# Routing chain of a mixture-of-experts kernel: transposing the residual raw, with norm factor and modulation moved behind the gather

## The chip, the cores and the metric

The kernel runs on one core of a Trainium2 chip. Its time is the device time of one execution in microseconds (us). The matrix engine is TensorE (PE; its weight loads are PEld), the others are VectorE (DVE), ScalarE (ACT) and GpSimd (POOL); SyncE (SP) issues the weight transfers. SBUF is the memory the engines work from, PSUM holds matmul results in eight tiles of 128 x 512 float32.

## The reference

Two layers act on 256 tokens of width 1024 and 256 context tokens. The first mixes with a gated MLP and a convolution and has a dense feed-forward part. The second has windowed attention and a mixture of eight experts, of which each token takes two. The change lies in the second layer, between the attention's residual and the experts:

```python
hl = rms_norm(xl, norm_ffn_g[li]) * (1 + sc2) + sh2
...
logits = (h @ router).astype(jnp.float32)
vals, idx = lax.top_k(logits, TOP_K)
wts = jax.nn.softmax(vals, axis=-1)
...
for e in range(N_EXPERTS):
    y = y + combine[..., e:e + 1] * swiglu(h, w1[e], w3[e], w2[e])
```

So the normalised value of token n and feature d is x[n,d] times a factor r[n] of the token, times a factor and plus a shift that depend on the feature alone.

## The kernel before

The program is a list of steps, written out in the order in which every engine is to issue; each engine works through its own part of that order. Weights come in pieces of 1 MB ("granules") from SP's queue into raw buffers, ten at most here, and are issued as soon as a buffer is free. A granule of a float32 matmul in three passes is first split: ScalarE casts it (L233), VectorE subtracts the cast from it (L211), and `mm3` (L262 to L264) multiplies high by high, high by low and low by high parts. The splitting runs up to three granules ahead.

The residual lies feature-major: `xt[k]` holds 128 features by 512 tokens, its first 256 columns are the latent tokens. `wo` (four steps) adds the attention's output to it, collects the squares and multiplies the raw residual with the prepared router weights (`logits`, L1276). Then four steps follow: an ada granule pair (modulation vectors of the layer's last part, L371), `route_a`, another pair, `route_b`.

`route_a` ends the logits and the norm: `SumSq.finish` sums over features on TensorE (L310), takes the reciprocal root on VectorE (L269 to L275) and multiplies it into two diagonal matrices (L316). `route_b` spreads the factor to all partitions with these (L321), scales the logits and takes the two best experts per token on VectorE (L1320 to L1331). Five small matmuls (L1334 to L1338) count, for each token and expert, the chosen tokens before it, and the total per expert; all write one PSUM tile. Eight times, VectorE multiplies a tile of the residual with the factor (L1343) and ScalarE applies scale and shift (L1345) into the unused half of `xt`. After the fourth of these, the rank is copied out (L1347), the one-hots for the first expert are built (L1440: place number equal to rank, times selection), and the order of the experts by size is worked out (`order_a`) and read into SP's registers (`order_load`), since it decides which weights are fetched next. Then sixteen 128 x 128 transposes (L1359) make the tokens lie on partitions, copied out (L1360) into `htok`.

`gather(n)` selects an expert's tokens by matmuls of `htok` with the one-hots (L1492): two halves of four feature blocks, 32 instructions in all, each half in one PSUM tile. ScalarE casts a half into the high part of `xg` (L1495), VectorE subtracts to get the low part (L1496). `gather(0)` stands in `route_b`; it is called again ahead of each of the three other experts with 128 places. The four experts with 64 places are served by one `gather_small` (L1505, L1506). For the large experts `eh` and `ey` run in three passes; the small ones use raw weights (L1550, L1607). In the sequence, pieces of a large and of a small expert alternate. Behind the last step stands a loop for the case that an expert has more tokens than places.

Of the kernel before, what the change touches and what calls it, by code (L numbers as in the profile page):

```python
# [22 lines left out]
F32 = mybir.dt.float32  # L23
# [4 lines left out]
AF = mybir.ActivationFunctionType  # L28
ALU = mybir.AluOpType
AX = mybir.AxisListType  # L30

P = 128
D = 1024
KD = 8
T = 512
L = 256
FF = 3584
NFG = 7
E = 8
# [47 lines left out]
def build(ctx, tc, io):  # L87
    nc = tc.nc
    ve, se, te = nc.vector, nc.scalar, nc.tensor
# [3 lines left out]
    cp = ctx.enter_context(tc.tile_pool(name="cp", bufs=1))  # L93
# [4 lines left out]
    pools = {"s": phase.enter_context(tc.tile_pool(name="sp", bufs=SB, side="right"))}  # L98
# [4 lines left out]
    cnt = [0]  # L103
# [5 lines left out]
    def S(dtype=F32):  # L109
        return pools["s"].tile([P, 512], dtype, tag="s", name=nm("s"))  # L110
# [7 lines left out]
    def PS():  # L118
        return pp.tile([P, 512], F32, tag="p", name=nm("p"))
# [7 lines left out]
    f32 = lambda ap: ap.bitcast(F32)  # L127


    vecs = cp.tile([P, NV], F32, name="vecs")  # L130
    ident = cp.tile([P, P], F32, name="ident")
    xt = [xp.tile([P, 512], F32, tag="xt", name=f"xt{k}") for k in range(KD)]
    cst = cp.tile([P, NK], F32, name="cst")
    rows = cp.tile([P, R_BS], F32, name="rows")
    router = cp.tile([P, KD, E], F32, name="router")
    ones = cp.tile([P, P], F32, name="ones")
# [8 lines left out]
    Affn = [cp.tile([P, KD, 2], F32, name=f"af{l}") for l in range(2)]  # L145
    SH1, SC1, G1, SH2, SC2, G2 = (8 * i for i in range(6))

    def mod(l, c, s):
        q = mpos(c)
        return modT[l][:, q, s:s + 1]  # L150
# [127 lines left out]
    def rsqrt(v, n):  # L278
        y = tiny(n)
        for op in rsqrt_ops(v, n, y):  # L280
            op()
        return y

    class SumSq:
# [17 lines left out]
        def add(self, src):  # L302
            self.accum(self.square(src))

        def finish(self):

            nt = self.n // P
            ps = PS()
            for t in range(nt):
                te.matmul(ps[:, t:t + 1], lhsT=self.acc[:, t * P:(t + 1) * P], rhs=ones[:, 0:1], start=True, stop=True)  # L310
            v = tiny(nt)
            ve.tensor_scalar(v, ps[:, :nt], 1.0 / D, EPS, op0=ALU.mult, op1=ALU.add)
            self.r = rsqrt(v, nt)
            self.dg = S()
            for t in range(nt):
                ve.tensor_scalar(self.dg[:, t * P:(t + 1) * P], ident, self.r[:, t:t + 1], None, op0=ALU.mult)  # L316
# [11 lines left out]
    C = {}  # L328
# [975 lines left out]
    def route_a(_):  # L1304
        logits(6)
        logits(7)
        C["ss"].finish()

    def route_b(_):
        pb = C["ss"].bcast()  # L1310
        r = C["ss"].r
        iota8 = iota[:, :E]
        sel = cp.tile([P, 2, E], F32, name="sel")
        comb = cp.tile([P, 2, E], F32, name="comb")
        rank = cp.tile([P, 2, E], F32, name="rank")
        lgs = tiny(16).rearrange("p (t e) -> p t e", t=2)
        mx = tiny(16).rearrange("p (t e) -> p t e", t=2)
        ix = tiny(16, U32).rearrange("p (t e) -> p t e", t=2)
        for t in range(2):
            ve.scalar_tensor_tensor(lgs[:, t, :], C["lg"][t][:, :E], r[:, t:t + 1], C["c0"], op0=ALU.mult, op1=ALU.add)  # L1320
            ve.max(mx[:, t, :], lgs[:, t, :])
            ve.max_index(ix[:, t, :], mx[:, t, :], lgs[:, t, :])
        del C["lg"]
        xf = tiny(4).rearrange("p (t c) -> p t c", t=2)
        ve.tensor_copy(xf, ix[:, :, 0:2])
        o0 = tiny(16).rearrange("p (t e) -> p t e", t=2)
        o1 = tiny(16).rearrange("p (t e) -> p t e", t=2)
        for t in range(2):
            ve.tensor_scalar(o0[:, t, :], iota8, xf[:, t, 0:1], None, op0=ALU.is_equal)
            ve.tensor_scalar(o1[:, t, :], iota8, xf[:, t, 1:2], None, op0=ALU.is_equal)  # L1330
        ve.tensor_add(sel, o0, o1)  # L1331
        tri = cst[:, K_TRI:K_TRI + P]
        ps = PS()
        te.matmul(ps[:, 0:E], lhsT=tri, rhs=sel[:, 0, :], start=True, stop=True)  # L1334
        te.matmul(ps[:, E:2 * E], lhsT=tri, rhs=sel[:, 1, :], start=True, stop=False)
        te.matmul(ps[:, E:2 * E], lhsT=ones, rhs=sel[:, 0, :], start=False, stop=True)
        te.matmul(ps[:, 2 * E:3 * E], lhsT=ones, rhs=sel[:, 0, :], start=True, stop=False)
        te.matmul(ps[:, 2 * E:3 * E], lhsT=ones, rhs=sel[:, 1, :], start=False, stop=True)  # L1338

        hn = []  # L1340
        for k in range(KD):
            t = S()
            ve.tensor_mul(t[:, :L], xt[k][:, :L], pb[:, :L])  # L1343
            hn.append(xt[k][:, L:])
            se.activation(hn[k], t[:, :L], AF.Identity, bias=mod(1, SH2 + k, 0), scale=Affn[1][:, k, 0:1])  # L1345
            if k == 3:
                ve.tensor_copy(rank, ps[:, 0:2 * E].rearrange("p (t e) -> p t e", t=2))  # L1347
                C["sel"], C["comb"], C["rank"] = sel, comb, rank
                onehots(0)
                cnt = C["cnt"] = cp.tile([P, E], F32, name="cnt")  # L1350
                ve.tensor_copy(cnt, ps[:, 2 * E:3 * E])
                order_a()
                order_load()
        htok = C["htok"] = pools["t"].tile([P, 2, D], F32, tag="htok", name="htok")
        for hf in range(2):
            for t in range(2):
                pt = PS()
                for k in range(4):
                    te.transpose(pt[:, k * P:(k + 1) * P], hn[4 * hf + k][:, t * P:(t + 1) * P], ident)  # L1359
                (se.copy if t else ve.tensor_copy)(htok[:, t, hf * 512:(hf + 1) * 512], pt)  # L1360
        gather(0)
        flush_tails()

        w = tiny(6).rearrange("p (c t) -> p c t", t=2)
        ve.tensor_sub(w[:, 0, :], mx[:, :, 1], mx[:, :, 0])
        se.activation(w[:, 0, :], w[:, 0, :], AF.Exp)
        ve.tensor_scalar(w[:, 1, :], w[:, 0, :], 1.0, None, op0=ALU.add)
        ve.reciprocal(w[:, 1, :], w[:, 1, :])
        ve.tensor_mul(w[:, 2, :], w[:, 0, :], w[:, 1, :])
        for t in range(2):  # L1370
            ve.tensor_scalar(o0[:, t, :], o0[:, t, :], w[:, 1, t:t + 1], None, op0=ALU.mult)
            ve.scalar_tensor_tensor(comb[:, t, :], o1[:, t, :], w[:, 2, t:t + 1], o0[:, t, :], op0=ALU.mult, op1=ALU.add)
# [48 lines left out]
    def order_load():  # L1421

        _, C["ex"] = nc.values_load_multi_w_load_instructions(
            C["exi"][0:1, :], engines=[mybir.EngineType.SP], min_val=1, max_val=E - 1)
        state["stop"] = None
        issue_dma()
# [8 lines left out]
    def onehots(n):  # L1435

        sel, _, rank = column(n)
        oh = S()
        for t in range(2):
            ve.tensor_scalar(oh[:, t * P:(t + 1) * P], iota, rank(t), sel(t), op0=ALU.is_equal, op1=ALU.mult)  # L1440
        C["oh"] = [oh[:, t * P:(t + 1) * P] for t in range(2)]
# [41 lines left out]
    def gather(n):  # L1483

        oh = C.pop("oh")
        xg = pools["t"].tile([P, 2, KD, P], F32R, tag="xg", name=nm("xg"))
        for hf in range(2):
            ps = PS()
            for kk in range(4):
                k = 4 * hf + kk  # L1490
                for t in range(2):
                    te.matmul(ps[:, kk * P:(kk + 1) * P], lhsT=C["htok"][:, t, k * P:(k + 1) * P], rhs=oh[t],  # L1492
                              start=(t == 0), stop=(t == 1), skip_group_check=True)
            pv = ps.rearrange("p (k c) -> p k c", k=4)
            se.copy(xg[:, 0, 4 * hf:4 * hf + 4, :], pv)  # L1495
            ve.tensor_sub(xg[:, 1, 4 * hf:4 * hf + 4, :], pv, f32(xg[:, 0, 4 * hf:4 * hf + 4, :]))  # L1496
        C["xg"] = [(xg[:, 0, k, :], xg[:, 1, k, :]) for k in range(KD)]

    def gather_small(_):

        oh = C.pop("ohs")
        for k in range(KD):
            ps = PS()
            for t in range(2):
                te.matmul(ps[:, :L], lhsT=C["htok"][:, t, k * P:(k + 1) * P], rhs=oh[t], start=(t == 0), stop=(t == 1))  # L1505
            se.copy(xt[k][:, L:], ps[:, :L])  # L1506

    ada(1, 10, quiet=True, late=True)
    step(route_a, quiet=True)
# [221 lines left out]
    with tc.If(cv > 0):  # L1731
        for t in range(2):
            ve.tensor_sub(rank[:, t, :], rank[:, t, :], C["slots"])
        with tc.For_i(0, E, 1) as ei:
# [17 lines left out]
            for k in range(KD):  # L1752
                ps = PS()
                for t in range(2):
                    te.matmul(ps[:, :P], lhsT=htok[:, t, k * P:(k + 1) * P], rhs=oh[:, t * P:(t + 1) * P],
                              start=(t == 0), stop=(t == 1))
                ve.tensor_copy(xg[k // 4][:, (k % 4) * P:(k % 4 + 1) * P], ps[:, :P])
            yp = [PS(), PS()]
            for fg in range(NFG):
                hp = []  # L1760
# [153 lines left out]
```

## Time and profile before

| | us |
|---|---|
| median of three runs | 1869.96 (1869.2 to 1872.01) |
| the profiled execution, its own time | 1878.57 |
| its span, first to last instruction | 1876.7 |

| engine | busy us | share of span |
|---|---|---|
| TensorE matmuls | 1785.8 | 95% |
| TensorE weight loads | 1300.2 | 69% |
| VectorE | 1133.6 | 60% |
| ScalarE | 768.1 | 41% |
| GpSimd | 438.7 | 23% |

Times in the rows below are from the start of the span. A busy share is an average over stages with different limits, so the stages have to be looked at one by one. An engine's wait is put down to whatever released it last.

### The profile page before, as it was taken

The page shows a single profiled execution, that of the slowest core. Times are in us where ns is not written, and L with a number is a line of the kernel's source. Part 1 is how long each engine was busy: PE and PEld are TensorE (multiplying, and loading weights), DVE is VectorE, ACT ScalarE, POOL GpSimd, SP SyncE. Part 2 cuts the span into 40 slices and gives each one's busy share as a digit, 9 for nine tenths or more (in the row PEclk, how much of TensorE's full clock was granted, in tenths as well). Part 3 has the DMA queues.
Part 4 walks back from the last instruction along what each step waited for, and adds up shares of the span by engine and source line. Part 5 has one row for each costly group of instructions (what it writes and reads, how often), then busy time and mean ns, then how long its engine had stood idle before and what let it go on. Part 6 is the DMA issues. An engine that isn't in the chain of part 4 may idle for free.

```text
span 1876.7 us, 24027 instructions
## 1 busy us (share of the span) xinstructions
PE 1785.8 (95%) x9438; PEld 1300.2 (69%) x9438; DVE 1133.6 (60%) x1598; ACT 768.1 (41%) x851; POOL 438.7 (23%) x188
## 2 busy tenths in 40 slices
PE   5999999999999999987989999999999999999998
PEld 4889878788888888886587656565656565656553
DVE  5788874378977521568757555655555545555553
ACT  4545543432222222254736444444443444444441
POOL 1587446245444444416600000000000000000000
PEclk8999999999999999998999999999999999999999
DMA  8542144554544422250076999999999999999994
GB/s 337 183 148 77 60 159 155 197 186 155 181 160 153 157 90 90 93 199 23 2 314 249 406 419 420 361 421 401 419 420 375 392 421 419 416 365 412 404 420 183
DMA packets 71686, 489.99 MB, mean 261 GB/s; under 512 B 8080, under 2 KB 9488, under 8 KB 13200
## 3 DMA queue, kind: packets, MB, share of 16 engines
q1 hardware_dynamic: 70992, 487.88, 65.9%
q8 instruction: 76, 1.25, 0.3%
q10 hardware_dynamic: 576, 0.52, 0.1%
q14 instruction: 42, 0.34, 0.1%
HBM read 487.32 MB, written 1.05 MB: 260 GB/s over the span
## 4 chain that ended last, share of the span: by engine, by line
PE 70%; DMA 12%; DVE 10%; ACT 4%; issue 3%; POOL 0%; SPq 0%; DVEq 0%; ACTq 0%; POOLq 0%
PE p L262 18%; PE p L264 17%; PE p L263 17%; DMA raw<-in_moe 9%; PE p L1550 8%; DVE lo L211 3%; PE p L1607 2%; ACT hi L233 2%; DMA q<-in_moe 2%; DVE p L569 1%; PE p L1570 1%; DVE s L300 1%; PE p L1176 1%; PE p L371 1%; PE p L1157 1%
## 5 line engine op out<-in xcount | busy, mean ns | idle before, releaser
L211 POOL TENSOR_TENSOR lo<-raw,hi 128x2048 fp32r<-128x2048 f32 (+1 forms) x68 | 309.4, 4553 | 426.1 <-ACT hi L233 406.9
L233 ACT CAST hi<-raw 128x2048 fp32r<-128x2048 f32 x172 | 327.7, 1907 | 188.4 <-PE p L264 80.3
L262 PE MATMUL p<-s,hi 128*128 128x512 f32 x960 | 376.2, 392 | 0.7 <-ACT s L434 0.7
L263 PE MATMUL p<-s,hi 128*128 128x512 f32 x960 | 374.8, 390 | 1.4 <-DVE s L764 1.1
L264 PE MATMUL p<-s,lo 128*128 128x512 f32 x960 | 374.5, 390 | 0.6 <-POOL lo L205 0.6
L211 DVE TENSOR_TENSOR lo<-raw,hi 128x2048 fp32r<-128x2048 f32 (+1 forms) x108 | 244.9, 2269 | 80.0 <-ACT hi L233 80.0
L211 DVE TENSOR_TENSOR lo<-q,hi 128x2048 fp32r<-128x2048 f32 x70 | 160.2, 2292 | 217.0 <-ACT hi L233 217.0
L233 ACT CAST hi<-q 128x2048 fp32r<-128x2048 f32 x70 | 133.4, 1907 | 187.9 <-DMA q<-in_moe 132.6
L262 PEld LDWEIGHTS p<-s,hi 128*128 128x128 f32 x960 | 180.9, 188 | 40.0 <-ACT s L434 0.9
L263 PEld LDWEIGHTS p<-s,hi 128*128 128x128 f32 x960 | 180.8, 188 | 39.8 <-DVE s L764 1.7
L264 PEld LDWEIGHTS p<-s,lo 128*128 128x128 f32 x960 | 180.8, 188 | 38.6 <-POOL lo L205 1.1
L264 PE MATMUL p<-hi,xg 128*128 128x512 f32 x448 | 176.8, 395 | 5.4 <-DVE xg L1496 5.4
L262 PE MATMUL p<-hi,xg 128*128 128x512 f32 x448 | 180.6, 403 | 0.0
L263 PE MATMUL p<-lo,xg 128*128 128x512 f32 x448 | 176.9, 395 | 2.2 <-DVE lo L211 2.1
L262 PE MATMUL p<-hi,s 128*128 128x256 f32 (+1 forms) x480 | 164.8, 343 | 1.6 <-ACT s L434 1.6
L263 PE MATMUL p<-lo,s 128*128 128x256 f32 (+1 forms) x480 | 160.8, 335 | 0.0
L397 DVE SCALAR_TENSOR_TENSOR s<-raw,o 128x512 f32<-128x512 f32 x128 | 158.8, 1303 | 0.0
L1550 PE MATMUL p<-q,xt 128*64 128x512 f32 x552 | 153.1, 613 | 0.0
L446 DVE SCALAR_TENSOR_TENSOR xt<-p,mod,xt 128x256 f32<-128x256 f32 x216 | 90.3, 476 | 76.9 <-PE p L264 69.6
L569 DVE SCALAR_TENSOR_TENSOR p<-s,vecs,p 128x494 f32<-128x494 f32 (+11 forms) x192 | 125.8, 732 | 6.2 <-ACT p L551 6.2
L264 PE MATMUL p<-hi,s 128*128 128x512 f32 (+1 forms) x352 | 123.7, 351 | 0.0
L262 PEld LDWEIGHTS p<-hi,s 128*128 128x128 f32 x480 | 92.3, 192 | 31.8 <-issue 21.9
(251 smaller groups left out, 2193.9 us busy)
## 6 DMA issues: line engine op xcount, KB each, us to landing
raw<-in_moe SPq DMA_DIRECT2D x181, 1024.0 KB, 10.2
q<-in_moe SPq DMA_DIRECT2D x153, 1024.0 KB, 14.0
raw<-in_ff SPq DMA_DIRECT2D x42, 1024.0 KB, 4.8
raw<-in_ada SPq DMA_DIRECT2D x31, 1024.0 KB, 5.8
raw<-in_adaT SPq DMA_DIRECT2D x16, 1024.0 KB, 4.8
raw<-in_w_ag SPq DMA_DIRECT2D x8, 1024.0 KB, 6.6
raw<-in_w_uv SPq DMA_DIRECT2D x8, 1024.0 KB, 4.8
raw<-in_w_out SPq DMA_DIRECT2D x6, 1024.0 KB, 4.8
```

The source lines that it names most:

```text
L211: eng.tensor_sub(lo[:, sl], r[:, sl], f32(hi[:, sl]))
L233: se.copy(hi, raws[i])
L262: te.matmul(out, lhsT=lh[0], rhs=rh[0], start=first, stop=False, skip_group_check=True)
L263: te.matmul(out, lhsT=lh[0], rhs=rh[1], start=False, stop=False, skip_group_check=True)
L264: te.matmul(out, lhsT=lh[1], rhs=rh[0], start=False, stop=last, skip_group_check=True)
L300: ve.tensor_add(self.acc[:, :n], self.acc[:, :n], q[:, :n])
L371: te.matmul(ps[32 * j:32 * j + 32, :P], lhsT=cpad[:, k, :], rhs=rv[:, kk, j * P:(j + 1) * P], start=(k == 0), stop=(k == 7), skip_group_ch ...
L397: ve.scalar_tensor_tensor(j, g[0][:, jj * D + q * 512:jj * D + (q + 1) * 512], 1.0, C["cb"][s][q], op0=ALU.mult, op1=ALU.mult, accum_out=h ...
L446: ve.scalar_tensor_tensor(xt[d][:, sl], ps[:, sl], mod(l, gbase + d, s), xt[d][:, sl], op0=ALU.mult, op1=ALU.add)
L569: ve.scalar_tensor_tensor(ov[:, :, lo:hi], gv[:, :, lo + s:hi + s], vecs[:, w0 + j:w0 + j + 1], ov[:, :, lo:hi], op0=ALU.mult, op1=ALU.add)
L1550: te.matmul(ps[SMALL * z:SMALL * (z + 1), :], lhsT=xt[k][:, o:o + SMALL], rhs=w[z][:, kk, :], start=(k == 0), stop=(k == 7), skip_group_ch ...
L1607: te.matmul(yps[n][SMALL * z:SMALL * (z + 1), :], lhsT=hT[:, f * SMALL:(f + 1) * SMALL], rhs=w[:, ff, z * 512:(z + 1) * 512], start=(fg == ...
```

## The change

The residual is transposed raw, at the start of `route_b`; the norm's factor is multiplied into the selection (`selr`), from which all one-hots are built; scale and shift are applied to the gathered rows. The diagonals and the spreading matmul are no longer made on this path. Counting is done by four matmuls, the totals in a PSUM tile of their own. In `gather` the modulation is made twice from the PSUM tile: by ScalarE into the high part, by VectorE in float32 into an SBUF tile `v`, from which the high part is subtracted. A filler of 448 bytes per partition and the new `selr` (64 bytes) shift later tiles by 512 bytes.

```diff
+    cp.tile([P, 112], F32, name="pad")
...
-        def finish(self):
+        def finish(self, diag=True):
...
             self.r = rsqrt(v, nt)
+            if not diag:
+                return
...
-        C["ss"].finish()
+        C["ss"].finish(diag=False)
+
+    def modulated(o, ps, k):
+
+        se.activation(o, ps, AF.Identity, bias=mod(1, SH2 + k, 0), scale=Affn[1][:, k, 0:1])
 
     def route_b(_):
-        pb = C["ss"].bcast()
         r = C["ss"].r
+        htok = C["htok"] = pools["t"].tile([P, 2, D], F32, tag="htok", name="htok")
+        for hf in range(2):
+            for t in range(2):
+                pt = PS()
+                for k in range(4):
+                    te.transpose(pt[:, k * P:(k + 1) * P], xt[4 * hf + k][:, t * P:(t + 1) * P], ident)
+                se.copy(htok[:, t, hf * 512:(hf + 1) * 512], pt)
...
+        selr = cp.tile([P, 2, E], F32, name="selr")
...
-        ps = PS()
-        te.matmul(ps[:, 0:E], lhsT=tri, rhs=sel[:, 0, :], start=True, stop=True)
-        te.matmul(ps[:, E:2 * E], lhsT=tri, rhs=sel[:, 1, :], start=True, stop=False)
-        te.matmul(ps[:, E:2 * E], lhsT=ones, rhs=sel[:, 0, :], start=False, stop=True)
-        te.matmul(ps[:, 2 * E:3 * E], lhsT=ones, rhs=sel[:, 0, :], start=True, stop=False)
-        te.matmul(ps[:, 2 * E:3 * E], lhsT=ones, rhs=sel[:, 1, :], start=False, stop=True)
-
-        hn = []
-        for k in range(KD):
-            t = S()
-            ve.tensor_mul(t[:, :L], xt[k][:, :L], pb[:, :L])
-            hn.append(xt[k][:, L:])
-            se.activation(hn[k], t[:, :L], AF.Identity, bias=mod(1, SH2 + k, 0), scale=Affn[1][:, k, 0:1])
...
+        ps, pc = PS(), PS()
+        te.matmul(ps[:, 0:2 * E], lhsT=tri, rhs=sel.rearrange("p t e -> p (t e)"), start=True, stop=False,
+                  skip_group_check=True)
+        te.matmul(ps[:, E:2 * E], lhsT=ones, rhs=sel[:, 0, :], start=False, stop=True, skip_group_check=True)
+        te.matmul(pc[:, 0:E], lhsT=ones, rhs=sel[:, 0, :], start=True, stop=False)
+        te.matmul(pc[:, 0:E], lhsT=ones, rhs=sel[:, 1, :], start=False, stop=True)
+        for t in range(2):
+            ve.tensor_scalar(selr[:, t, :], sel[:, t, :], r[:, t:t + 1], None, op0=ALU.mult)
+        ve.tensor_copy(rank, ps[:, 0:2 * E].rearrange("p (t e) -> p t e", t=2))
+        C["sel"], C["comb"], C["rank"] = selr, comb, rank
+        onehots(0)
+        cnt = C["cnt"] = cp.tile([P, E], F32, name="cnt")
+        ve.tensor_copy(cnt, pc[:, 0:E])
+        order_a()
+        order_load()
         gather(0)
         flush_tails()
...
-            pv = ps.rearrange("p (k c) -> p k c", k=4)
-            se.copy(xg[:, 0, 4 * hf:4 * hf + 4, :], pv)
-            ve.tensor_sub(xg[:, 1, 4 * hf:4 * hf + 4, :], pv, f32(xg[:, 0, 4 * hf:4 * hf + 4, :]))
+            v = S()
+            for kk in range(4):
+                k, pk = 4 * hf + kk, ps[:, kk * P:(kk + 1) * P]
+                modulated(xg[:, 0, k, :], pk, k)
+                ve.tensor_scalar(v[:, kk * P:(kk + 1) * P], pk, Affn[1][:, k, 0:1], mod(1, SH2 + k, 0), op0=ALU.mult,
+                                 op1=ALU.add)
+            ve.tensor_sub(xg[:, 1, 4 * hf:4 * hf + 4, :], v.rearrange("p (k c) -> p k c", k=4),
+                          f32(xg[:, 0, 4 * hf:4 * hf + 4, :]))
...
-            se.copy(xt[k][:, L:], ps[:, :L])
+            modulated(xt[k][:, L:], ps[:, :L], k)
```

The loop behind the last step gets `modulated` in place of its copy as well.

## Rows read from the trace of the kernel before

**Rows 1.** Stretches: us, busy time (instructions) per engine, TensorE clock, DMA share, GB/s.
```profile
970.00:989.20 19.20, 14.43 (x131) 12.14 (x131) 11.40 (x51) 6.05 (x12) 0.00 (x0) 0.73 0.59 229
...
1200.00:1300.00 100.00, 99.48 (x458) 62.08 (x458) 55.60 (x44) 41.87 (x33) 0.00 (x0) 1.00 0.95 384
1300.00:1400.00 100.00, 93.94 (x428) 55.13 (x426) 57.77 (x43) 46.57 (x35) 0.00 (x0) 1.00 1.01 419
```

**Rows 2.** Timeline, 969 to 985: start, us, what, count, [idle before, releaser].
```profile
971.68 1.08 PE L371 MATMUL p<-q,cpad 128*32 128x128 f32 x32
...
973.09 0.48 DVE L316 TENSOR_SCALAR s<-ident,t 128x128 f32<-128x128 f32 x2
...
976.27 0.59 PE L1334 MATMUL p<-sel,cst 128*128 128x8 f32 x2 [1.94 <-DVE sel L1331]
...
978.00 0.57 PE L1338 MATMUL p<-sel,ones 128*128 128x8 f32 x2
...
978.61 0.17 DVE L1347 COPY rank<-p 128x16 f32<-128x16 f32 x1 [1.07 <-PE p L1338]
978.82 0.60 DVE L1440 TENSOR_SCALAR s<-cst,rank,sel 128x128 f32<-128x128 f32 x2
...
984.51 13.23 SPq L185 DMA_DIRECT2D q<-in_moe  x4
...
984.88 4.46 PE L1492 MATMUL p<-s,htok 128*128 128x128 f32 x32
```

**Rows 3.** Timeline, from the first gather to the first weight subtractions.
```profile
989.20 0.47 PE L262 MATMUL p<-hi,xg 128*128 128x512 f32 x1
...
989.99 0.69 DVE L1496 TENSOR_TENSOR xg<-p,xg 128x512 fp32r<-128x512 f32 x1 [1.09 <-ACT xg L1495]
...
990.97 3.70 ACT L233 CAST hi<-q 128x2048 fp32r<-128x2048 f32 x2
...
992.89 6.70 DVE L211 TENSOR_TENSOR lo<-q,hi 128x2048 fp32r<-128x2048 f32 x3 [0.42 <-ACT hi L233]
```

**Rows 4.** Timeline around the gather of the second large expert.
```profile
1187.91 3.73 PE L1492 MATMUL p<-s,htok 128*128 128x128 f32 x32
...
1190.48 0.59 ACT L1495 CAST xg<-p 128x512 fp32r<-128x512 f32 x1
...
1190.98 2.28 DVE L211 TENSOR_TENSOR lo<-raw,hi 128x2048 fp32r<-128x2048 f32 x1
...
1193.92 0.50 PE L264 MATMUL p<-hi,xg 128*128 128x512 f32 x1 [1.81 <-DVE xg L1496]
```

**Rows 5.** The chain of waits, same place: start, us, what.
```profile
1193.18 0.69 DVE xg L1496
...
1196.31 0.43 PE p L264
...
1227.57 12.34 DMA q<-in_moe
```

**Rows 6.** Stretches of 2 us behind this gather, columns as in rows 1.
```profile
1196.00:1198.00 2.00, 2.00 (x6) 1.51 (x6) 0.00 (x0) 0.00 (x0) 0.00 (x0) 0.50 0.99 410
...
1208.00:1210.00 2.00, 2.00 (x12) 0.57 (x8) 2.00 (x3) 0.79 (x1) 0.00 (x0) 1.00 0.18 25
```

**Rows 7.** Timeline of TensorE: four transposes in the experts.
```profile
1088.48 0.66 PE L1570 MATMUL p<-ident,s 128*128 128x128 f32 x4 [1.07 <-DVE s L1535]
```

**Rows 8.** Single lines: count, ns min/median/max, first and last start, forms.
```profile
L379 ACT COPY s<-p x16: 247/265/266, 18.3 to 972.8; 128x128 f32<-128x128 f32 x16
...
L1345 ACT ACTIVATE xt<-s,mod,af x8: 585/586/600, 976.6 to 983.1; 128x256 f32<-128x256 f32 x8
...
L1506 ACT COPY xt<-p x8: 366/372/382, 1022.1 to 1027.2; 128x256 f32<-128x256 f32 x8
...
L1440 DVE TENSOR_SCALAR s<-cst,by,by x6: 340/342/343, 1150.4 to 1587.5; 128x128 f32<-128x128 f32 x6
...
L446 DVE SCALAR_TENSOR_TENSOR xt<-p,mod,xt x216: 467/475/485, 244.6 to 1870.0; 128x256 f32<-128x256 f32 x108
```

More of the change, by code (lines that the diff above doesn't have):

```diff
@@ L1341, in route_b @@
-        for k in range(KD):
-            t = S()
-            ve.tensor_mul(t[:, :L], xt[k][:, :L], pb[:, :L])
-            hn.append(xt[k][:, L:])
-            se.activation(hn[k], t[:, :L], AF.Identity, bias=mod(1, SH2 + k, 0), scale=Affn[1][:, k, 0:1])
[L1346 to L1360, printed above, removed]
+        ps, pc = PS(), PS()
+        te.matmul(ps[:, 0:2 * E], lhsT=tri, rhs=sel.rearrange("p t e -> p (t e)"), start=True, stop=False,
+                  skip_group_check=True)
@@ L1756, in build @@
                               start=(t == 0), stop=(t == 1))
-                ve.tensor_copy(xg[k // 4][:, (k % 4) * P:(k % 4 + 1) * P], ps[:, :P])
+                modulated(xg[k // 4][:, (k % 4) * P:(k % 4 + 1) * P], ps[:, :P], k)
             yp = [PS(), PS()]
```

## The prediction

> **What bounds the kernel now.** I read the stretches first, because the change sits in two kinds of place: once between attention and experts, and once per expert with 128 places. From 970 to 989.2 us [rows 1] TensorE is busy 14.4 of 19.2 us at a granted clock of 0.73 and the DMA engines at 0.59: neither works at its limit, a chain of small steps does. In the experts the DMA share is 1.01 in one stretch of 100 us, with TensorE busy 94, and 0.95 in another, with TensorE busy 99 [rows 1]: two limits take turns, with little slack left in either.
>
> Second, the timeline of the routing chain [rows 2]. TensorE ends its last ada matmuls at 972.8. VectorE builds the diagonal (0.48), reads logits and makes the selection; five counting matmuls run from 976.27 to 978.57; only then is the rank copied (978.61), and the one-hots end at 979.4. The gather matmuls begin at 984.9, because they wait for tokens that are normalised, modulated and transposed in between. Third, what follows them [rows 3]: the second subtraction of the gather ends at 990.7, ScalarE takes up the next weight cast at 990.97, and VectorE the first of three weight subtractions in a row at 992.89. That start is the mark by which I count the gain.
>
> Fourth, the gather inside the experts. One of the three is shown [rows 4]; the other two repeat it. The gather's matmuls take 3.73 us; VectorE is held by a weight subtraction until 1193.2, then does the gather's subtraction, and TensorE stands 1.81 us for it. The chain of waits goes through this place [rows 5]: subtraction, TensorE, and 34 us later a weight transfer. The two stretches of 2 us [rows 6] show why a delay here isn't absorbed: the granted clock has fallen to 0.50 behind the wait, and at 1208 the DMA share is 0.18, so the transfers stand still too until buffers come free.
>
> **The change part by part.** *The routing chain.* Without the diagonal the selection comes about 0.45 us earlier, so the counting matmuls start at 975.8. The sixteen transposes now come before them and need only the residual: four take 0.66 us [rows 7], all 2.6 us, from 972.8 to 975.4, and end in time. Their four copies on ScalarE cost 0.59 each by the 512-wide copy in [rows 4], with nothing else on that engine; the last is done near 976. The rank now waits for two matmuls of 0.46 instead of five: 976.8. The two multiplications of the selection by the factor (0.2 each, estimated from the 0.17 us rank copy in [rows 2]) fit into that wait. Rank 0.2, one-hots 0.6 [rows 2]: the gather matmuls start at 977.6 instead of 984.7, 7.1 us earlier. The 8 multiplications and 8 modulations of whole tiles are gone from the path.
>
> *The expert order.* It follows the one-hots on VectorE; these come 1.8 us earlier (979.4 to 977.6), so SP's reads of the order and the first four transfers of a chosen expert behind them (984.51 in [rows 2]) do too. These weights are used only after 120 matmuls of the fixed expert, over 25 us behind its first at 0.21 each, so this buys and costs nothing.
>
> *The first gather itself.* Before, one cast (0.59) and one subtraction (0.69) per half. After: four ScalarE modulations, four VectorE ones and a subtraction per half, and both engines read the same PSUM tile. No row shows two engines reading one PSUM tile. The nearest is the rank copy [rows 2]: its 16 columns were ready after three matmuls (977.7), yet it started after the fifth, which writes 8 other columns of that tile. Waits go by the whole tile. I take it that the two engines' readings take turns in the order written: ScalarE, VectorE, ScalarE, VectorE.
>
> The Trainium skill, "PSUM — Partial Sum Buffer", section "PSUM bank collisions raise a hardware error", says that ScalarE and VectorE must not access one bank at once, reads against reads included. By it the turns are forced and the sum is the one below; without it the sum is the first rival's. No run here shows it.
>
> Prices. ScalarE: a 128x128 copy out of PSUM takes 0.265; scale and bias by pointer and the other side cost 0.586-0.372=0.21 on 256 columns [rows 8]; so 0.47 (bounds 0.37 and 0.59). VectorE: 0.342 for 128 columns in SBUF with two pointers, 0.475 for 256 out of PSUM [rows 8]; I take the middle, 0.41. Two handovers of 0.04 (the counting matmuls' end to the rank copy [rows 2]). One turn is 0.96 us (0.78 to 1.1).
>
> The Trainium skill, "VectorE: DVE Perf Modes", section "Why PSUM operands drop a tier", says that a float32 operation on PSUM loses the double rate that it has in SBUF. By it the SBUF row grows by an estimated 0.07, to 0.41; by the row alone the result is 0.07 x 4 turns x 3 gathers = 0.8 us lower.
>
> First half: the gather's matmuls took 3.73 in [rows 4] and 4.46, partly at the half clock, in [rows 2], so a half about 2.0 and ends at 977.6+2.0=979.6; four turns 3.84 and the subtraction 0.69 give 984.1. Second half: VectorE modulates (0.45), three turns (2.9), subtraction: 988.1. Before it was 990.7. TensorE needs the first half at its third matmul and the second twelve matmuls later, so it waits at both; but the weight cast and the row of subtractions start 2.6 us earlier, at 988.4 and 990.3, and those are the limit there. Gain of the route: 2.6 us (1 to 4.5).
>
> *The three later gathers.* VectorE is free at 1193.2. Before: subtraction, TensorE at 1193.92. After: 0.41 + three turns 2.9 = 3.3 us more in front of the subtraction, TensorE at about 1197.2 (bounds 2.7 and 3.6 more). TensorE's wait grows from 1.8 to 5.1 us. The half clock cost it about 1.7 before (eight matmuls at 0.43 [rows 5], twice their time at the full clock). It may now last one stretch longer, or, if it doesn't, the second half's subtraction comes about 1.2 late: I take 0.5 more (-0.5 to 1.7). So 3.8 each, 11.4 for three.
>
> *The rest.* The small experts' gather swaps 8 copies of 0.372 for modulations of at most 0.59; they start 0.73 us apart on average [rows 8], so they stay hidden, but for 0.2 at the last. The loop behind the last step isn't run here. The filler and the new small tile shift addresses by 512 bytes in all; the trace offers no price, and I put it at 0 within 1 us.
>
> Sum: -2.6 + 11.4 = +8.8 us. The profiled execution took 1878.57 (span 1876.7 and 1.9 around it) and lies 8.6 above the median of the runs, 1869.96; by it the new one would be 1887.4, by the median 1878.8. I predict 1878.8.
>
> **The rivals.** *Side by side.* If the two engines read one PSUM tile at once and follow the matmuls column block by column block, the first gather ends with its matmuls: TensorE starts the experts at 981.7 instead of 989.2, and VectorE's row starts 7.2 earlier. Each later gather then costs only VectorE's four modulations back to back, 0.26 to 0.30 each by the pair of one-hots (0.60 for two, [rows 2]), and some clock: 1.4, three times 4.2. Sum -3.0: 1867.0, not slower, which is the other side. For it: the operations read disjoint data. Against: the rank copy's wait. It decides from a delay per gather under 2.6/3 = 0.9 us, if the route gains no more than I think.
>
> *Absorbed.* The transfers run at share 1.01 in most of the experts [rows 1]; were they the only limit, a later TensorE at the gather would cost nothing, and the route's 2.6 stand alone: 1867.4. Against it: the 0.18 at 1208 [rows 6] and the chain [rows 5].
>
> *The transposes don't move up.* If their PSUM tiles or the token tile's space come free only after the logits are read, transposes and counting queue behind each other on TensorE, the gather starts about 3 us later than I say, and the route loses 0.4 instead of gaining: 1881.8. For it: eight PSUM tiles, two of them held by the logits until VectorE has read them; against: the others were done by 973.
>
> **How the numbers follow.** Turns: 0.76. Side by side: 0.10. Absorbed: 0.06. Transposes late: 0.06. Something else, such as the addresses: 0.02. Less than 0.2% (3.7 us) can't be told from no change here: faster is below 1866.2, slower above 1873.7. Within the first case the bounds give -4.5+3x2.7=3.6 to -1+3x5=14, so 1873.6 to 1884. Slower: 0.76 x 0.94 + 0.06 = 0.77 with part of the last case. Same: 0.04 of the first, half of the second, most of the third: 0.15. Faster: 0.08. The range must reach to the other cases to hold 8 in 10 with a margin for what was mis-sized: 1868 to 1885; the likeliest case alone is 1873.6 to 1884.
>
> **What would show it.** Right, if in the new trace ScalarE's and VectorE's operations of the gather alternate without overlap, the first weight subtraction of the experts lies 1 to 4.5 us nearer to the last ada matmul than 20.1 us (992.89-972.8), and TensorE waits about 5 us at each later gather. The step on the transposes is right if they end before the counting matmuls begin, and the one on the count if the rank copy follows the second of these. Wrong, if the two engines' rows overlap on one PSUM tile, if the waits at the gathers stay near 2 us, or if they grow and the chain no longer passes through them.

## Result and the profile after

The changed kernel takes 1881.54 us (median of five runs, 1875.27 to 1883.27) against 1869.2 (1866.02 to 1872.01): ratio 1.0058, 95% interval 1.0041 to 1.0074. Run again on another occasion it gave 1.0052 (1.0031 to 1.0073). It is slower by about 10 to 12 us; 8.8 were forecast.

The two profiled executions tell this badly if one looks at their spans: 1873.4 us after, 1876.7 before. The traced execution of after was the fastest of its five (1875.27), that of before (1878.57) lay above all five of its runs. So I compare stretches, not spans, and use every trace of the same form. The stretches of 19 and of 100 us, columns as in [rows 1]:

```profile
970.00:989.20 19.20, 13.13 (x74) 10.66 (x75) 13.53 (x40) 9.76 (x14) 0.00 (x0) 1.00 0.45 171
...
1200.00:1300.00 100.00, 100.00 (x460) 60.22 (x458) 55.90 (x45) 43.67 (x34) 0.00 (x0) 1.00 0.97 389
1300.00:1400.00 100.00, 95.98 (x428) 57.61 (x427) 55.12 (x43) 44.08 (x34) 0.00 (x0) 0.98 1.01 419
```

In this trace TensorE's clock isn't halved in the routing chain (1.00 against 0.73 in [rows 1]); the experts look the same as before on this scale. The timeline of the chain after, columns as in [rows 2]; the last ada matmuls end at 967.9 here, 972.8 before:

```profile
966.79 1.08 PE L374 MATMUL p<-q,cpad 128*32 128x128 f32 x32
967.81 1.97 PE L1323 MATMUL p<-ident,xt 128*128 128x128 f32 x16
...
971.10 0.37 PE L1348 MATMUL p<-sel,cst 128*128 128x16 f32 x2 [1.33 <-DVE sel L1345]
971.31 0.37 PE L1350 MATMUL p<-sel,ones 128*128 128x8 f32 x2
...
971.72 0.17 DVE L1355 COPY rank<-p 128x16 f32<-128x16 f32 x1 [0.37 <-PE p L1350]
971.93 0.60 DVE L1441 TENSOR_SCALAR s<-cst,rank,selr 128x128 f32<-128x128 f32 x2
972.42 3.84 PE L1493 MATMUL p<-s,htok 128*128 128x128 f32 x32 [0.29 <-DVE s L1441]
...
974.51 0.46 ACT L1314 ACTIVATE xg<-p,mod,af 128x128 fp32r<-128x128 f32 x1 [3.91 <-PE p L1493]
975.01 0.41 DVE L1499 TENSOR_SCALAR s<-p,af,mod 128x128 f32<-128x128 f32 x1 [0.63 <-ACT xg L1314]
975.45 0.46 ACT L1314 ACTIVATE xg<-p,mod,af 128x128 fp32r<-128x128 f32 x1 [0.48 <-DVE s L1499]
975.94 0.41 DVE L1499 TENSOR_SCALAR s<-p,af,mod 128x128 f32<-128x128 f32 x1 [0.53 <-ACT xg L1314]
...
978.26 0.69 DVE L1501 TENSOR_TENSOR xg<-s,xg 128x512 fp32r<-128x512 f32 x1
979.01 0.51 PE L265 MATMUL p<-hi,xg 128*128 128x512 f32 x1 [2.17 <-DVE xg L1501]
...
982.13 0.69 DVE L1501 TENSOR_TENSOR xg<-s,xg 128x512 fp32r<-128x512 f32 x1
...
983.11 5.49 ACT L234 CAST hi<-q 128x2048 fp32r<-128x2048 f32 x3
985.03 6.70 DVE L212 TENSOR_TENSOR lo<-q,hi 128x2048 fp32r<-128x2048 f32 x3 [0.42 <-ACT hi L234]
```

The gather matmuls begin 4.55 us behind the last ada matmul instead of 12.1: the chain itself became 7.6 us shorter. Then ScalarE (L1314) and VectorE (L1499) alternate on the PSUM tile without overlap, one turn every 0.94 us, and each waits for the other. The first weight subtraction, the mark of [rows 3], lies 17.2 us behind the last ada matmul instead of 20.1. Of 7.6 us, 3.0 are left.

The gather of [rows 4] after:

```profile
1180.11 3.73 PE L1493 MATMUL p<-s,htok 128*128 128x128 f32 x32
...
1183.18 2.29 DVE L212 TENSOR_TENSOR lo<-raw,hi 128x2048 fp32r<-128x2048 f32 x1
1185.38 0.41 DVE L1499 TENSOR_SCALAR s<-p,af,mod 128x128 f32<-128x128 f32 x1
1185.82 0.46 ACT L1314 ACTIVATE xg<-p,mod,af 128x128 fp32r<-128x128 f32 x1 [2.68 <-DVE s L1499]
...
1188.63 0.69 DVE L1501 TENSOR_TENSOR xg<-s,xg 128x512 fp32r<-128x512 f32 x1
...
1189.38 0.79 PE L265 MATMUL p<-hi,xg 128*128 128x512 f32 x1 [5.07 <-DVE xg L1501]
```

VectorE is freed by the weight subtraction at 1185.4 and starts its turns only there; TensorE waits 5.07 us instead of 1.81. What follows in stretches of 2 us, and the chain of waits, as in [rows 6] and [rows 5]:

```profile
1189.00:1191.00 2.00, 1.62 (x4) 1.33 (x5) 1.06 (x3) 0.84 (x2) 0.00 (x0) 0.50 1.00 414
1191.00:1193.00 2.00, 2.00 (x7) 1.52 (x6) 1.33 (x3) 0.53 (x2) 0.00 (x0) 0.50 1.02 422
...
1202.00:1204.00 2.00, 2.00 (x11) 0.78 (x11) 2.00 (x1) 1.73 (x2) 0.00 (x0) 1.00 0.14 57
```

```profile
1186.32 0.42 DVE s L1499
1186.76 0.47 ACT xg L1314
...
1188.63 0.70 DVE xg L1501
```

The granted clock is at 0.50 behind the wait, the lower of its two levels (1.2 of 2.4 GHz), and 13 us later the transfers run dry (0.14), as before; the chain now goes through the turns themselves.

All traces of either form side by side, in us. "Mark" is the distance from the end of the last ada matmul to the first weight subtraction; "to gather 2" that to the first matmul of the second large expert's gather; "rest" from there to the end of the span. The two kernels of the lower lines come from the experiments and have the same form behind the ada matmuls.

| form | trace | up to last ada matmul | mark | to gather 2 | rest |
|---|---|---|---|---|---|
| before | first | 972.8 | 20.1 | 215.1 | 688.8 |
| before | second | 968.7 | 18.9 | 213.9 | 684.3 |
| before | e10_shift64 | 984.8 | 21.4 | 216.8 | 681.7 |
| after | first | 967.9 | 17.2 | 212.2 | 693.3 |
| after | second | 969.9 | 17.9 | 212.6 | 697.4 |
| after | e4_nofill | 984.8 | 17.6 | 212.3 | 693.6 |

Means: mark 20.15 and 17.55, to gather 2 215.3 and 212.4, rest 684.9 and 694.7. The route gained 2.9 us, the rest lost 9.8: 7.0 in all by the traces, 10 to 12 by the medians. Traces of one form differ by up to 7 us in the rest, so the missing 3 to 5 us aren't located. Which executions were traced can make such a gap: those of before lie on average 2.8 us above the medians of their runs, those of after 2.1 below.

### The profile page after: what moved, and what is told of

The parts are those of the page before. It is cut to its first block, busy times and chain, and to the rows that moved or that the text cites. A ratio compares the mean times of both kernels' runs of the same rounds, so it can differ in the third digit from the quotient of the medians.

```text
span 1873.4 us, 24059 instructions
## 1 busy us (share of the span) xinstructions
PE 1777.9 (95%) x9434; PEld 1294.0 (69%) x9434; DVE 1140.7 (61%) x1620; ACT 775.8 (41%) x869; POOL 437.9 (23%) x188
## 4 chain that ended last, share of the span: by engine, by line
PE 68%; DMA 12%; DVE 11%; ACT 4%; issue 3%; POOL 0%; SPq 0%; DVEq 0%; ACTq 0%; POOLq 0%
PE p L263 17%; PE p L265 17%; PE p L264 17%; DMA raw<-in_moe 11%; PE p L1556 8%; DVE lo L212 4%; ACT hi L234 3%; PE p L1613 2%; DMA q<-in_moe 1%; DVE p L572 1%; PE p L1576 1%; DVE s L301 1%; PE p L1179 1%; PE p L374 1%; DVE s L1541 1%
## 5 line engine op out<-in xcount | busy, mean ns | idle before, releaser
L400 DVE SCALAR_TENSOR_TENSOR s<-raw,o 128x512 f32<-128x512 f32 x128 | 158.8, 1302 | 0.0
```

Source lines behind the costliest of these rows:

```text
L400: ve.scalar_tensor_tensor(j, g[0][:, jj * D + q * 512:jj * D + (q + 1) * 512], 1.0, C["cb"][s][q], op0=ALU.mult, op1=ALU.mult, accum_out=h ...
```

## Experiments

The theory ("turns"): the loss is the alternation of two engines on one PSUM tile at the gathers. The rival: it comes from half-clock stretches or from addresses, as the first pair of traces differs by only 1.6 us behind the ada matmuls (903.9 and 905.5).

**Both kernels again.**

> The changed kernel once more, unedited, for a second trace on the same chip as the next three. Both theories: the ratio to before again near 1.006 (1.003 to 1.008). Theory of turns: TensorE again waits 5.1 us at each of the three later gathers, and the stretch from the last ada matmul to the first weight subtraction is again about 17.2 us; whatever the runs differ in lies elsewhere. Rival (the loss is made by half-clock stretches or by addresses, since behind the last ada matmul the first trace of after is only 1.6 us longer than that of before): the waits are the same, but the stretch from the last ada matmul to the end differs from the first trace's 905.5 us by several us.

> The kernel before once more, unedited, for a second trace, since the profiled execution of the first lay 8.6 us above the median of its runs. Ratio 1.000. Both theories: TensorE waits 1.81 us at each later gather and 20.1 us lie between the last ada matmul and the first weight subtraction. If the first trace was slow behind the ada matmuls by chance, that stretch (903.9 us) is now some 5 to 9 us shorter; if it was slow ahead of them, the stretch is the same and the time up to them (972.8) shorter.

Ratios 1.0052 and 1.0008 (0.9991 to 1.0026). TensorE waits three times 5.1 and three times 1.8 us. The table above holds their stretches. The second trace of before is 4.1 us shorter up to the last ada matmul and 5.8 behind it, so its first was slower on both sides; the second of after is 4.4 longer behind it.

**Blocks of four instead of turns.**

```diff
                 modulated(xg[:, 0, k, :], pk, k)
+            for kk in range(4):
+                k, pk = 4 * hf + kk, ps[:, kk * P:(kk + 1) * P]
                 ve.tensor_scalar(v[:, kk * P:(kk + 1) * P], pk, ...
```

> The gather's four ScalarE modulations of a half all stand ahead of its four VectorE ones, nothing else is changed: the engines hand the PSUM tile over once per half instead of seven times. Theory of turns: at the later gathers VectorE's four run back to back behind the weight subtraction that holds it, so TensorE's wait falls from 5.07 to about 3.1 us (four at 0.30 and the subtraction 0.69 behind 1185.4), three times 2 us; the first gather ends about 2 us earlier; the time is 6 to 8 us below after, ratio to before 1.001 to 1.003. Rival (clock or addresses): no change against after, ratio 1.005 to 1.007.

Ratio 0.9995 (0.9981 to 1.0008), below the 1.001 to 1.003 expected: the loss is gone. The order of eight instructions per half is all that differs. The timeline of its gather:

```profile
1179.79 2.91 ACT L1314 ACTIVATE xg<-p,mod,af 128x128 fp32r<-128x128 f32 x8
...
1182.49 1.36 DVE L1501 TENSOR_SCALAR s<-p,af,mod 128x128 f32<-128x128 f32 x4
1183.88 0.69 DVE L1503 TENSOR_TENSOR xg<-s,xg 128x512 fp32r<-128x512 f32 x1
...
1184.63 0.50 PE L265 MATMUL p<-hi,xg 128*128 128x512 f32 x1 [3.22 <-DVE xg L1503]
```

ScalarE's eight are all but done when VectorE is through with the weights, VectorE's four then take 1.36 instead of 3.2, and the wait is 3.22, as expected; the mark is at 14.5. So of the 3.26 us by which the change lengthened each wait, the turns are 1.85; the other 1.41 are VectorE's four operations, which stand in front of its subtraction in either order. The median fell by 11 us, more than the 6 to 8 that I had worked out from the waits. By the traces, the way behind the last ada matmul is 7.8 us shorter than the mean of after (899.3 against 907.1), which is what the waits and the mark give; the clock has no part in that, as it is halved behind all three of these waits too.

**The new chain with the old gather.**

```diff
-            v = S()
-            for kk in range(4):
...
+            pv = ps.rearrange("p (k c) -> p k c", k=4)
+            se.copy(xg[:, 0, 4 * hf:4 * hf + 4, :], pv)
+            ve.tensor_sub(xg[:, 1, 4 * hf:4 * hf + 4, :], pv, f32(xg[:, 0, 4 * hf:4 * hf + 4, :]))
```

> The changed kernel with the gather of before, one ScalarE cast and one VectorE subtraction per half: scale and shift of the large experts' rows are left out of the computation. It shows what the new routing chain is worth when the gather costs what it did. Theory of turns: the first weight subtraction comes 7 us nearer to the last ada matmul than before (about 13 us instead of 20.1), TensorE waits 1.81 us at the later gathers, ratio 0.996 (1862). Rival: the gather is not what costs, so the ratio stays between 1.003 and 1.007.

Ratio 0.9946 (0.9926 to 0.9965). The mark is at 12.0 us (979.00 by the row below, behind 967.05), so the chain is worth 8 us at the mark when nothing is given back; the way from there to the 17.6 of after is the first gather's turns.

```profile
979.00 2.29 DVE L212 TENSOR_TENSOR lo<-q,hi 128x2048 fp32r<-128x2048 f32 x1 [0.42 <-ACT hi L234]
```

**The old chain with the new gather.**

```diff
-            pv = ps.rearrange("p (k c) -> p k c", k=4)
-            se.copy(xg[:, 0, 4 * hf:4 * hf + 4, :], pv)
-            ve.tensor_sub(xg[:, 1, 4 * hf:4 * hf + 4, :], pv, f32(xg[:, 0, 4 * hf:4 * hf + 4, :]))
+            v = S()
+            for kk in range(4):
+                k, pk = 4 * hf + kk, ps[:, kk * P:(kk + 1) * P]
+                se.activation(xg[:, 0, k, :], pk, AF.Identity, bias=cpad[:, k, 2:3], scale=ones[:, k:k + 1])
+                ve.tensor_scalar(v[:, kk * P:(kk + 1) * P], pk, ones[:, k:k + 1], cpad[:, k, 2:3], op0=ALU.mult,
+                                 op1=ALU.add)
+            ve.tensor_sub(xg[:, 1, 4 * hf:4 * hf + 4, :], v.rearrange("p (k c) -> p k c", k=4), ...
```

> The kernel before, routing chain and modulation untouched, with only the gather's new form: each half is read in four turns by ScalarE and VectorE, here with scale 1 and shift 0. Theory of turns: TensorE waits 5.1 us instead of 1.8 at the three later gathers, and the first weight subtraction comes about 5 us later than before (25 instead of 19 to 20 behind the last ada matmul); 5 + 3x3 = 14 us in all, ratio 1.006 to 1.009. Rival (clock or addresses of the changed kernel): the form of the gather alone costs less than 4 us, ratio below 1.002.

Ratio 1.0108 (1.0091 to 1.0125), above the 1.006 to 1.009 expected. Its waits of TensorE (line, releaser: us in total, times, longest) and its first weight subtraction, 25.1 us behind the last ada matmul at 967.39:

```profile
PE p L264 <- DVE xg L1500: 15.2, 3, 5.1
```

```profile
992.49 4.49 DVE L211 TENSOR_TENSOR lo<-q,hi 128x2048 fp32r<-128x2048 f32 x2 [0.43 <-ACT hi L233]
```

Waits and mark are those of the theory. The traced execution, the fastest of its five, lies 14.7 us above the median of before, where 14 were expected; the median lies 21.4 above, and the 7 us between them aren't explained. With e2_copy the parts add up: the chain alone makes the kernel faster by 0.5%, the new gather alone slower by 1.1%, both together slower by 0.5 to 0.6%.

**Without the filler.**

```diff
-    cp.tile([P, 112], F32, name="pad")
```

> The changed kernel without the filler, so later tiles lie 64 bytes instead of 512 behind their places of before. Theory of turns: addresses have no price that can be measured, ratio 1.003 to 1.007 like after, waits and distances as in after. Rival (addresses): the time differs from after by more than 4 us, and durations of VectorE or ScalarE instructions on moved tiles differ.

Ratio 1.0119 (1.0102 to 1.0135): the rival is right for this one. It lost another 11 us, but not at the gathers (15.1 us of waits, the mark at 17.6): the time up to the last ada matmul is 984.8 instead of 969.9. The stretch 500 to 600 us, in the dense matmuls of the first layer, of the second trace of after and then of this kernel:

```profile
500.00:600.00 100.00, 100.00 (x443) 82.84 (x442) 79.42 (x140) 23.53 (x20) 44.12 (x10) 1.00 0.43 153
```

```profile
500.00:600.00 100.00, 100.00 (x431) 80.59 (x430) 67.42 (x130) 22.92 (x19) 43.46 (x10) 1.00 0.43 152
```

At the same clock, 443 matmuls in 100 us became 431: 0.226 to 0.232 us each. VectorE's durations differ too, as the rival said, but they fall: the 128 x 512 operations of L400 in after take 1.23 us on average between 300 and 900 us, instead of 1.30.

**64 bytes in front of the kernel before.**

```diff
+    cp.tile([P, 16], F32, name="pad")
     xt = [xp.tile([P, 512], F32, tag="xt", name=f"xt{k}") for k in range(KD)]
```

> The kernel before with 64 bytes per partition put in front of its tiles, nothing else. Theory of addresses (for what e4_nofill showed): the weight parts now lie as in e4_nofill, the dense matmuls of the first layer follow each other at 0.232 us instead of 0.226 (431 instead of 443 in 100 us), the last ada matmul ends some 13 to 17 us later, ratio 1.006 to 1.009, and the part behind it is as before. Rival: e4_nofill lost its time by something else in its code, ratio here within 0.998 and 1.002.

Ratio 1.0077 (1.0058 to 1.0096), 984.8 us to the last ada matmul, 898.5 behind it. Nothing but addresses differs, and the stretch shows the same count:

```profile
500.00:600.00 100.00, 100.00 (x431) 80.59 (x430) 67.42 (x130) 22.92 (x19) 43.43 (x10) 1.00 0.44 152
```

So a shift by 64 bytes costs 14 us in this kernel and the filler keeps that away. It isn't what made the change slower: after has the filler, and its way to the last ada matmul (967.9 and 969.9) is that of before (972.8 and 968.7).

**Gathers issued ahead of the next weight group.** VectorE's weight subtraction in front of the gather [rows 4] is there because the step splits the next weights first. Marked `quiet`, the step doesn't; the next one does.

```diff
-            step(lambda g, m=seq[i + 1][0]: gather(m))
+            step(lambda g, m=seq[i + 1][0]: gather(m), quiet=True)
```

With the blocks of four:

> The blocks of four as in e1_blocks, and the later gathers issued ahead of the cast and subtraction of the next weight group instead of behind them. Theory of turns, with VectorE's order as what is left at the gathers: TensorE's wait there falls from 3.2 to about 1.6 us, three times 1.6, ratio 0.996 to 0.998. Rival: the weight group that is now split later takes the place of the wait removed (TensorE then waits for a weight subtraction 24 matmuls further on), ratio 0.999 to 1.001 as for e1_blocks.

On the kernel before alone:

> The kernel before with only the later gathers issued ahead of the next weight group's cast and subtraction. Theory of turns, which puts the gain of e5_both over before to the routing chain and the issue order: TensorE's wait of 1.81 at each later gather falls below 1 us, three times about 1, ratio 0.997 to 0.999, and the routing chain as before. Rival: the issue order makes the whole gain of e5_both, ratio 0.994.

Ratios 0.9941 (0.9926 to 0.9955) and 0.9949 (0.9935 to 0.9964). Both lie below what was expected, and the second's rival came close: the issue order alone makes most of the gain. With the blocks TensorE's wait is 1.5 us at each later gather, as expected:

```profile
PE p L265 <- DVE xg L1503: 4.4, 3, 1.5
```

In the kernel before with the new order no wait for the gather is left, and the clock isn't halved there (the same place, the kernel before in its second trace first, then the one with the new order):

```profile
1184.00:1188.00 4.00, 2.75 (x23) 2.31 (x21) 3.97 (x5) 2.29 (x3) 0.00 (x0) 1.00 1.03 426
1188.00:1192.00 4.00, 3.44 (x9) 2.77 (x10) 1.10 (x2) 0.00 (x0) 0.00 (x0) 0.64 1.02 422
```

```profile
1184.00:1188.00 4.00, 4.00 (x33) 3.81 (x32) 3.52 (x3) 2.37 (x4) 0.00 (x0) 1.00 1.02 422
1188.00:1192.00 4.00, 4.00 (x22) 3.40 (x22) 2.25 (x4) 2.82 (x3) 0.00 (x0) 1.00 1.01 420
```

I had priced the wait (1.8) and not what can follow it: nine matmuls took 3.44 us of TensorE's time in these 4 us; at 0.23 each they take 2.1, so 1.3 to 1.4 us more are lost there. This loss doesn't come each time. In the same trace of before, the clock stays at 1.00 behind the same wait of 1.81 us at the next large expert (6 us from the end of the wait, first one, then the other):

```profile
1188.50:1194.50 6.00, 5.94 (x19) 4.75 (x20) 0.60 (x2) 1.76 (x1) 0.00 (x0) 0.72 1.02 422
1408.90:1414.90 6.00, 6.00 (x28) 4.72 (x29) 1.98 (x2) 2.19 (x2) 0.00 (x0) 1.00 1.01 418
```

From the matmul that waits to the twentieth behind it, the nine later gathers in the three traces of before's form take 5.74 us on average: about 6.3 at the six where the clock is halved, 4.7 at the other three. With the new order they take 4.56. Three times the wait of 1.8 and this loss of 1.2 is 9.0; the median fell by 9.7. For the blocks, the same stretch takes 6.70 us on average with the old order (e1_blocks, halved at all three) and 4.70 with the new (at 1.00 at all three); three times this and the 1.75 us of shorter wait is 11, and the time fell by 10 to 11.

**ScalarE alone on the PSUM tile.** As e5_both, with ScalarE modulating into SBUF and VectorE casting and subtracting from there.

```diff
-                modulated(xg[:, 0, k, :], pk, k)
-                ve.tensor_scalar(v[:, kk * P:(kk + 1) * P], pk, ...
+                modulated(v[:, kk * P:(kk + 1) * P], ps[:, kk * P:(kk + 1) * P], 4 * hf + kk)
...
+            ve.tensor_copy(xg[:, 0, 4 * hf:4 * hf + 4, :], v)
...
```

> As e5_both, but ScalarE alone reads the gather's PSUM tile (four modulations of 0.35 into SBUF), and VectorE casts and subtracts from SBUF, at about 0.4 and 0.69 per half. Theory of turns: no handover is left; TensorE waits about 1 us at the later gathers, the first weight subtraction is about 13.5 us behind the last ada matmul, ratio 0.994 to 0.997. Rival: what e1_blocks left over isn't at the gathers, no difference from e5_both.

Ratio 0.9930 (0.9915 to 0.9946), 1857.7 us: faster than both kernels, and a little below the 0.994 to 0.997 expected, though the mark is at 15.0 instead of 13.5. The wait is nearly gone:

```profile
PE p L263 <- DVE xg L1499: 0.8, 3, 0.3
```

Against e5_both and e6_bquiet the intervals overlap; so it isn't shown that it beats these.

**The routing weights later.** The exponential and the operations behind it are emitted at the head of `order_b`.

```diff
...
+        C.pop("weights")()
         perm = C["ord"][:, 1, :].rearrange("p (a b) -> p a b", a=NR7)
```

> As e9_actquiet, with the routing weights (an exponential and six small VectorE operations) moved from behind the first gather to the step that first reads them. Theory: the first weight cast no longer waits for VectorE's last gather subtraction and the exponential, so the first weight subtraction comes 1 to 1.5 us earlier; ratio 0.992 against 0.993, near what can be told. Rival: VectorE is busy with the same operations a little later and PE waits there, no change.

Ratio 0.9946 (0.9931 to 0.9961). The mark moved from 15.0 to 11.8 us, more than expected (in e9_actquiet the first gather's matmuls had run 5.47 us at a partly halved clock, so not all of it is the edit), and the time shows nothing of it.

## Why the prediction was right

Direction, size and mechanism held; the time lay 2.7 us above the forecast. Two things were off: the clock's term was about half of what came, and a gain elsewhere had no term. That they nearly cancel is luck.

- *The turns.* One turn was put at 0.96 us and took 0.94: ScalarE 0.457, VectorE 0.410 and two handovers.

```profile
L1499 DVE TENSOR_SCALAR s<-p,af,mod x32: 403/410/411, 975.0 to 1633.9; 128x128 f32<-128x128 f32 x32
```

```profile
L1314 ACT ACTIVATE xg<-p,mod,af x32: 448/457/461, 974.5 to 1633.4; 128x128 fp32r<-128x128 f32 x32
```

 In the stretches shown, no two of them overlap on one PSUM tile. The Trainium skill, "PSUM — Partial Sum Buffer", section "PSUM bank collisions raise a hardware error", forbids two engines on one bank at once, reads included; the trace shows an order that obeys it, though not what would happen without. VectorE's price is 0.07 above its 0.342 of [rows 8] in SBUF. The Trainium skill, "VectorE: DVE Perf Modes", section "Why PSUM operands drop a tier", says that float32 operands in PSUM leave VectorE at its single rate; the 0.07 agrees with the estimate that the prediction made by it.
- *The chain.* Transposes ended at 969.8, ahead of the counting matmuls at 971.1; the rank copy followed the second of these (the wait of 0.37 for L1350); the gather came 7.6 us earlier (6.6 against the second trace of before), 7.1 were forecast. The route's gain at the mark was 2.6 us by the means of three traces each, as forecast. Side by side and late transposes are excluded by the rows above.
- *The later gathers.* The wait grew by 3.26 us, forecast 3.3. For the clock 0.5 per gather was taken; it was 0.95: behind the 5.1 us it is halved at all nine later gathers of the three traces, behind the 1.8 at six of nine, and the way to the twentieth matmul behind the wait takes 6.69 us instead of 5.74. Three gathers so cost 12.6, and 11.4 were forecast. The rest of the span grew by only 9.8. The sum had no term for the difference: TensorE's waits for VectorE's tile `s` ahead of the experts' transposes (L1570 of before) fell from 17.1 to 14.6 us behind the second gather's start, in traces that differ among themselves by up to 3.7. The rival "absorbed" is excluded: the delay reaches the end.
- *The sum.* -2.6 + 11.4 = 8.8 stands against -2.9 + 9.8 = 7.0 by traces (from unrounded means) and 10 to 12 by medians.
- *What I sized badly.* The price of a wait: 0.5 us per gather for the clock was a guess, about half of what came, and e6_bquiet gained more than its waits. Two numbers of the working don't hold: the gather before starts at 984.88 in [rows 2], not 984.7, and the prices' own upper bounds make a later gather 0.475 + 3 x 1.1 = 3.8 us dearer at most, not 3.6; neither changes the forecast. And the addresses: "0 within 1 us" was right only because the filler stands there.

## What to carry to other kernels

Where two engines' instructions on one PSUM tile alternate in the program, the engines took turns here: issue one engine's whole block first, or let one engine read and the other work from SBUF. Before work is moved off a chain that runs once, look whether it lands in a place that runs several times with its own wait; here 7.6 us were won once, of which the first gather gave back 5 and three more took 3.3 each, and about 1 each by the clock. And look at what stands in front of a waiting instruction on its engine: issuing the gather ahead of a weight subtraction was worth as much as the whole restructured chain (0.9949 and 0.9946).

## What the hardware showed beyond that

The addresses of tiles count for TensorE: with everything behind it 64 bytes further on, the same matmuls at the same granted clock of 1.00 followed each other at 0.232 instead of 0.226 us, some 14 us up to the last ada matmul, in two kernels. Which of the moved tiles does it was not tried.

A wait can cost more than itself, and not each time: behind 1.8 us of idle TensorE the clock was halved at six of nine places and stayed at 1.00 at three, with the same wait and the same instructions. Behind the 5.1 us of after it was halved at all nine, behind the 1.5 of e5_both and without a wait at none of three.
